# mLSTM and HGRN2 step on one Trainium2 core: the heads' normalised rows turned by VectorE and DRAM in place of TensorE

## The chip, the cores and the metric

One core of one Trainium2 chip. The metric is the time of one execution of the whole program on the device, in microseconds (us); three runs of the kernel before give a median of 1104.61 (1103.64 to 1105.09).

The engines named below work side by side, each through its own list of instructions in order: TensorE (PE; its weight loads are shown as PEld), VectorE (DVE), ScalarE (ACT), GpSimd (POOL) and SyncE (SP). SP issues nearly all DMAs here.

## The reference

One inference step of a layer with two parallel branches, for 512 prompt tokens and 32 sample tokens (544 together). Only the mLSTM branch matters here: four heads of 512 channels.

```python
def _head_layernorm(h, g):
    mu = jnp.mean(h, axis=-1, keepdims=True)
    d = h - mu
    y = d * lax.rsqrt(jnp.mean(d * d, axis=-1, keepdims=True) + EPS)
    return y.reshape(h.shape[0], h.shape[1], -1) * g
...
hm, C_new, n_new, m_new = _mlstm(qm, km, vm, ig, lf, C0, n0, m0)
hm = _head_layernorm(hm.transpose(0, 2, 1, 3), mnorm_g[l])
hm = (hm + m_skip[l] * c) * jax.nn.silu(z_m)
ya = hm.astype(x.dtype) @ w_brm[l]
```

c is the convolved and activated input of the head, z_m a gate, and ya the branch's output, summed over the heads. Everything is float32.

## The kernel before, in words

**Layout.** Nearly everything is held turned: channels on the 128 partitions, the 544 tokens along the free axis (32 sample tokens first, then 512 of the prompt), so a head is KH = 4 tiles f of 128x544. A product of float32 matrices is made of three matmuls: each operand is split into a high half (a cast on ACT, line 146 for rows, 204 for weights) and a low half (a subtraction on DVE, line 147 or 205). Names end in h and l: hm4h and hm4l are the halves of hm tile 4, ws210h and ws210l those of a sum of projection weights.

**Heads.** mchain(h, pump) computes head h = 0 to 3. It is a generator: each `yield n` lets `pump` put n steps of the *next* projection units on PE (line 575; six matmuls a step) before the head goes on. So PE's list is a mixture written by hand: a piece of the head, some projection, a piece of the head. The orders of ACT, DVE and SP come from the scheduler, by the program's order, its priorities and the times it reckons with; they are fixed when the program is built.

**The place that changes.** A head's output comes out with tokens on partitions: five tiles y, four of 128x512 (prompt) and one of 32x512 (sample). They are normalised in place, tiles 1 and 3 by ACT (line 1345), 0, 2 and 4 by DVE (line 1347). To meet c and z they must be turned to channels on partitions. For each f, five matmuls against the identity (lines 1366, 1367) write a PSUM tile yt, and DVE adds it, times the norm's weight, into c: line 1372 for the prompt, 1373 for the sample. Line 1374 multiplies by z, and split gives hm.

- Heads 1 and 2 first run memory(h, f) for their new state (96 matmuls, line 1112; the results Co go out by SP at line 1128) and then the projection steps KWGAP[2] = 11. Heads 0 and 3 wait GAPS[h] = 20 or 14 steps.
- stage_br(h) follows with the ya matmuls (line 229): eight units of 24 matmuls, each over all four hm tiles. A unit begins with hm tile 0 and the weights wbm; from head 1 on DVE adds earlier heads' sums (line 1392), which travel through DRAM (ya_d).
- Between a head's chain and its ya come the last projection units of that stage. Their weights are loaded by SP, cast by ACT and subtracted on DVE, in the same lists as the hm work.
- Behind head 3 the HGRN2 part begins. Its first activations tf, hq and hkq need three different function tables on ACT (ACT_TABLE_LOAD).

**Turning through DRAM is in the kernel already.** For heads 1 to 3 the rows kf are turned by `turn` (line 975: DVE transposes blocks of 32 by 32 in place; line 979: SP writes the blocks to DRAM, k_d, 16 DMAs a head), and read back at lines 1155 and 1164.

Of the kernel before, what the change touches and what calls it, by code (L numbers as in the profile page):

```python
# [9 lines left out]
F32 = mybir.dt.float32  # L10
# [4 lines left out]
ALU = mybir.AluOpType  # L15

P = 128
D = 1024
KD = D // P
NS = 32  # L20
NP = 512
T = NS + NP
TH = T // 2
FAR, NEAR = 48, 4
MH = 4
HD = 512
KH = HD // P
HH = 8
NB = NP // P
# [12 lines left out]
PDGAP = 1  # L42
VGAPS = (0, 0, 0, 0)
ZN = 3
FIRSTK, KTGAP, KWGAP = (3, 2, 1, 1, 1), (6, 14), (6, 3, 11)
VTGAP = ((2, 1, 1, 1, 1), (1, 1, 1, 1, 1), (1, 1, 1, 1, 1), (0, 2, 2, 1, 1))
GAPS = (20, 20, 20, 14)
APART = 10
FDELAY = (2, 2, 5)
QDELAY = 2  # L50
# [33 lines left out]
def hybrid_step(ctx: ExitStack, tc: tile.TileContext, a, o):  # L84
    nc = tc.nc
    V, S, G, PE = nc.vector, nc.scalar, nc.gpsimd, nc.tensor
# [20 lines left out]
    dr = ctx.enter_context(tc.tile_pool(name="dr", bufs=1, space=bass.MemoryType.DRAM))  # L107
    pd = ctx.enter_context(tc.tile_pool(name="pd", bufs=4, space=bass.MemoryType.PSUM))

    def slot(name, dt=F32):  # L110
        return sp.tile([P, WP + P // 2], dt, tag="s", name=name)
# [26 lines left out]
    def paux(name):  # L138
        return psum["a"].tile([P, 2, 512], F32, tag="a", name=name)
# [141 lines left out]
    ident = cp.tile([P, P], F32, name="ident")  # L281
# [822 lines left out]
    def memory(h, f, kw, vv, pool=paux):  # L1104
# [23 lines left out]
        nc.sync.dma_start(o["Cp"][h, f], co[:, :VW])  # L1128
        yield

    v_d = dr.tile([NB, 2, P, VW], F32, name="v_d")
    k_d = [dr.tile([T, HD], F32, name=f"k_d{h}") for h in range(MH)]

    def mchain(h, pump):

        t = st8[h]
# [69 lines left out]
        for b in range(NB):  # L1206
            yield VTGAP[h][b]
            pt = paux(f"vt{h}{b}")
# [10 lines left out]
        pt = paux(f"vts{h}")  # L1219
# [56 lines left out]
        yb = []  # L1276
        olds += [old(2), old(3)]

        def sample():
            pn = paux(f"nm{h}{NB}")  # L1280
            for f in range(KH):
                ch, cl = olds[f]
                last = f == KH - 1
                for g in range(2):
                    v, d = VS[g], slice(VP[g], VP[g] + VN[g])
                    if last:
                        PE.matmul(pn[:NS, g, d], dss, vs[:, v], start=False, stop=False)
                    for x, m in ((1, 1), (0, 2)) if last else ((0, 2), (1, 1)):
                        PE.matmul(
                            pn[: m * NS, g, d],  # L1290
                            qw[:, f, :m].rearrange("p o t -> p (o t)"),
                            (ch, cl)[x][:, v],
                            start=(f == 0 and x == 0),
                            stop=(last and x == 0),
                        )
            ysm = slot(f"y{h}{NB}")
            G.memset(ysm[:, :HD], 0.0)
            with tc.high_priority():
                S.copy(ysm[:NS, :VW], joined(pn)[:NS])
                yl = slot(f"yl{h}")  # L1300
                S.copy(yl[:NS, :VW], joined(pn)[NS : 2 * NS])
                V.tensor_tensor(ysm[:NS, :VW], ysm[:NS, :VW], yl[:NS, :VW], ALU.add)
                numbers(NB, NS, ysm)
            return ysm

        for i in range(NB):
            if i == NB - 1:
                ysm = sample()
# [13 lines left out]
            y = slot(f"y{h}{i}")  # L1322
# [5 lines left out]
        n5 = NB + 1  # L1328
        with tc.high_priority():
# [11 lines left out]
            for i in range(n5):  # L1341
                p = P if i < NB else NS
                y = yb[i][:p, :HD]
                if i % 2:
                    S.activation(y, y, AF.Identity, scale=rs[:p, i : i + 1], bias=mrs[:p, i : i + 1])
                else:
                    V.tensor_scalar(y, y, stt[:p, i, 0:1], rs[:p, i : i + 1], ALU.subtract, ALU.mult)

        if 0 < h < MH - 1:
            for b in range(NB):  # L1350
                fetch(b)
            yield KWGAP[0]
            for b in range(NB):
                parted(b)
            yield KWGAP[1]
            for f in range(KH):
                for _ in memory(h, f, kw, vv):
                    pass

        hs = []  # L1360
        for f in range(KH):
            yield max((KWGAP[2] if 0 < h < MH - 1 else GAPS[h]) if f == 0 else 1, pump.when["z", f] - pump.done)
            ft = h * KH + f
            pt = paux(f"yt{ft}")
            for b in range(NB):
                PE.transpose(pt[:, 0, b * P : (b + 1) * P], yb[b][:, f * P : (f + 1) * P], ident)
            PE.transpose(pt[:, 1, :P], yb[NB][:, f * P : (f + 1) * P], ident)
            c, (z, act) = t["cc"][f], t["z"][f]
            with tc.issue_after(act.ins):
                S.mul(c[:, :T], c[:, :T], vcol(V_SK + ft))  # L1370
            g = vcol(V_MG + ft)
            V.scalar_tensor_tensor(c[:, NS:T], pt[:, 0, :], g, c[:, NS:T], ALU.mult, ALU.add)
            V.scalar_tensor_tensor(c[:, :NS], pt[:, 1, :NS], g, c[:, :NS], ALU.mult, ALU.add)
            V.tensor_tensor(c[:, :T], c[:, :T], z[:, :T], ALU.mult)
            hs.append(split(c[:, :T], f"hm{ft}"))
        t["hs"] = hs
# [68 lines left out]
    with tc.manual_schedule(engines={mybir.EngineType.Activation, mybir.EngineType.DVE, mybir.EngineType.PE}):  # L1445
# [15 lines left out]
        for k in range(KD):  # L1461
            t = xt[k]
            hi, lo = far_pair("x0", k)
            g = t[:, T : T + 1]
# [10 lines left out]
            if k in (3, 4):  # L1475
                i = 2 * (k - 3)
                V.tensor_tensor(sq[i], sq[i], sq[i + 1], ALU.add)
            if k in (5, 6):
                i, j = ((0, 2), (4, 5))[k - 5]
# [9 lines left out]
        r = rms_cols(sq[0][:, :T], [(0, NS)] + [(NS + b * P, P) for b in range(NB)], "r0", pc)  # L1489
# [106 lines left out]
        pump = Pump(fill(0))  # L1596
# [103 lines left out]
    with tc.manual_schedule(engines={mybir.EngineType.PE}):  # L1700
        for h in range(MH):
# [16 lines left out]
            else:  # L1718
                pump = Pump(fill(h))
# [271 lines left out]
    with tc.manual_schedule(engines={mybir.EngineType.PE}):  # L1991
        pump = Pump(list(hgrn), staged=True)
# [17 lines left out]
    for k in range(2):  # L2010
        t = slot(f"p{k}")
# [46 lines left out]
    for k in range(KD // 2):  # L2058
        for f in (k, k + KD // 2):
            w = weight(a["w_brh"][f], f"wbh{f}", at=spread())  # L2060
            acc = dense(w, 0, P, P, obs, f"yb{f}")
            t = gbs[f]
# [191 lines left out]
```

## Time and profile before

| | |
|---|---|
| median of three runs | 1104.61 us |
| the profiled execution's own time | 1106.07 us |
| its span, first to last instruction | 1104.3 us |
| TensorE clock granted, mean | 0.999 |
| line 1366 and 1367, matmuls on PE | 64 and 16 |
| line 1112, matmuls of memory() | 288 |

Times in the rows are us from the span's start. A row of a timeline has start, length, engine, line, operation, output<-inputs, form and count, and in brackets how long the engine sat idle before it and what released it. A row of one tile or one line gives minimum, median and maximum of one instruction in ns, then the first and last start. A row of the waits is engine, tile and line, then what it waited for: total us, times, longest.

### The profile page before, as it was taken

How to read it: one execution, taken by the hardware profiler on the slowest of the kernel's cores; microseconds unless marked ns; L12 is line 12 of the kernel's file. 1: busy time of each engine (PE TensorE's matmuls, PEld its weight loads, DVE VectorE, ACT ScalarE, POOL GpSimd, SP SyncE). 2: the span in 40 equal slices, each digit the busy share in tenths (PEclk: the TensorE clock that was granted, in tenths of full speed). 3: DMA queues.
4: the chain of work that ended last, by engine and by line, in shares of the span. 5: the costliest groups of instructions: out<-in, count | busy, mean ns of one | idle time of the engine just before them, and what ended most of it. 6: DMA issues, size and time to landing. Idle time of an engine off the chain costs nothing.

```text
span 1104.3 us, 23737 instructions
## 1 busy us (share of the span) xinstructions
PE 1089.9 (99%) x8765; PEld 1077.4 (98%) x8765; DVE 920.8 (83%) x1989; ACT 712.2 (64%) x1571; POOL 173.0 (16%) x417
## 2 busy tenths in 40 slices
PE   9999999999999999999999999999999999999998
PEld 9999999999999999999999999999999999999998
DVE  6986999679798596986898688999999888789885
ACT  6686656755666455664566478887777767445762
POOL 2122024111010130101100123322332100000000
PEclk9999999999999999999999999999999999999999
DMA  6223225634365344464556222122221353343743
GB/s 224 78 96 107 83 86 174 146 100 127 105 206 160 81 147 144 126 225 92 157 159 218 95 78 84 56 80 80 85 75 62 111 178 116 116 124 116 260 146 121
DMA packets 104781, 138.67 MB, mean 126 GB/s; under 512 B 35765, under 2 KB 43573, under 8 KB 104665
## 3 DMA queue, kind: packets, MB, share of 16 engines
q1 hardware_dynamic: 104496, 137.10, 40.0%
q8 instruction: 69, 1.13, 0.4%
q14 instruction: 48, 0.39, 0.1%
q10 hardware_dynamic: 168, 0.06, 0.0%
HBM read 110.96 MB, written 26.16 MB: 124 GB/s over the span
## 4 chain that ended last, share of the span: by engine, by line
PE 59%; DVE 12%; ACT 7%; issue 2%; DMA 0%; POOL 0%; DVEq 0%; ACTq 0%; POOLq 0%
PE d L575 26%; PE ya L229 6%; PE pg L2099 4%; PE yb L229 4%; PE C L1112 3%; PE q L229 3%; DVE ws L533 2%; PE k L229 2%; PE sc L1054 2%; DVE hkq L1836 2%; PE nm L1313 2%; PE ple L229 1%; DVE at L1852 1%; DVE ws L508 1%; ACT shared L1947 1%
## 5 line engine op out<-in xcount | busy, mean ns | idle before, releaser
L592 ACT COPY t<-d 128x272 f32<-128x272 f32 x126 | 47.5, 377 | 20.8 <-PE d L575 20.7
L1770 ACT COPY kmos<-hkq 128x256 f32<-128x256 f32 x56 | 23.9, 427 | 38.0 <-DVE hkq L1836 34.7
L1836 DVE TENSOR_TENSOR hkq<-hkq,hq 128x288 f32<-128x288 f32 (+1 forms) x96 | 41.4, 438 | 1.5
L1815 PE MATMUL pl<-hkq,kmos 128*128 128x128 f32 x224 | 35.5, 279 | 3.3 <-DVE hkq L1653 1.9
L801 DVE SCALAR_TENSOR_TENSOR cv<-ub,vec,cv 128x547 f32<-128x547 f32 x48 | 37.1, 782 | 0.4
L1815 PEld LDWEIGHTS pl<-hkq,kmos 128*128 128x128 f32 x224 | 30.0, 188 | 4.9 <-ACT kmos L1770 1.5
L1112 PE MATMUL C<-vh,kwl 128*128 128x256 f32 x96 | 27.0, 281 | 0.0
L1112 PE MATMUL C<-vl,kwh 128*128 128x256 f32 x96 | 26.9, 280 | 0.0
L1112 PE MATMUL C<-vh,kwh 128*128 128x256 f32 x96 | 26.8, 279 | 0.0
L1392 DVE TENSOR_TENSOR y<-ya,y 128x272 f32<-128x272 f32 x48 | 18.8, 434 | 8.0 <-PE ya L229 7.8
L1852 DVE COPY_PREDICATED at<-lmask,pl 128x256 f32<-128x256 uint8 x56 | 25.0, 446 | 0.0
L1313 PE MATMUL nm<-vh,sh 128*128 128x256 f32 x80 | 22.8, 285 | 1.0 <-ACT Co L1124 0.6
L1324 ACT COPY y<-nm 128x516 f32<-128x516 f32 x16 | 9.4, 588 | 21.5 <-PE nm L1313 21.5
L1313 PE MATMUL nm<-vl,sh 128*128 128x256 f32 x80 | 22.6, 282 | 0.0
L963 POOL COPY vsm<-vt 128x96 f32<-128x96 f32 x16 | 12.8, 809 | 62.2 <-DVE vt L599 43.9
L1313 PE MATMUL nm<-vh,sl 128*128 128x256 f32 x80 | 22.5, 281 | 0.0
L1068 ACT CAST sh<-dm 128x512 fp32r<-128x512 f32 (+3 forms) x16 | 7.4, 459 | 22.8 <-DVE dm L1062 22.8
L1054 PE MATMUL sc<-q,kh 128*128 128x512 f32 (+3 forms) x80 | 18.6, 321 | 0.0
L1243 DVE SCALAR_TENSOR_TENSOR c<-c,wi,Cs 128x256 f32<-128x256 f32 (+1 forms) x32 | 14.9, 471 | 4.1 <-PE Cs L1241 4.0
L1112 PEld LDWEIGHTS C<-vh,kwh 128*128 128x128 f32 x96 | 18.1, 189 | 0.0
L1112 PEld LDWEIGHTS C<-vl,kwh 128*128 128x128 f32 x96 | 18.1, 188 | 0.0
L1112 PEld LDWEIGHTS C<-vh,kwl 128*128 128x128 f32 x96 | 18.0, 188 | 0.0
(5767 smaller groups left out, 5164.6 us busy)
## 6 DMA issues: line engine op xcount, KB each, us to landing
ya_d<-y SPq DMA_DIRECT2D x32, 272.0 KB, 3.1
y<-ya_d SPq DMA_DIRECT2D x24, 272.0 KB, 3.1
c<-in_C SPq DMA_DIRECT2D x16, 258.0 KB, 3.6
out_Cs<-c SPq DMA_DIRECT2D x16, 258.0 KB, 2.6
out_Cp<-Co SPq DMA_DIRECT2D x15, 258.0 KB, 2.5
k_d<-kf SPq DMA_DIRECT2D x48, 68.0 KB, 2.0
x<-in_xT SPq DMA_DIRECT2D x8, 272.5 KB, 4.6
ya<-ya_d SPq DMA_DIRECT2D x8, 272.0 KB, 4.7
```

The costliest lines, as they stand in the source:

```text
L229: PE.matmul(both[b][:m, :TH], part(w, off + k * step, m, x), xx[:, half(b)], start=(k == 0 and j == 0), stop=(k == n - 1 and j == 2),)
L575: PE.matmul(ps, ww[:, c], xx, start=(start and k == 0 and j == 0), stop=end, skip_group_check=not start,)
L592: S.copy(t, ps)
L801: last = V.scalar_tensor_tensor(cv[:, :547], ub[:, j : j + 547], vcol(V_CW + 4 * ft + j), cv[:, :547], ALU.mult, ALU.add)
L1054: PE.matmul(pn[:, 0, :n], ks[f][x][:, j * P : (j + 1) * P], qs[f][y][:, NS + j * P : T], start=(f == 0 and i == 0), stop=(f == KH - 1 and ...
L1112: PE.matmul(pn[g], kw[b][x][:, f * P : (f + 1) * P], vv[b][y][:, VS[g]], start=(b == 0 and j == 0), stop=(b == NB - 1 and j == 2),)
L1313: PE.matmul(pn[:, g, VP[g] : VP[g] + VN[g]], st[j][x][:, (i - j) * P : (i - j + 1) * P], vv[j][y][:, VS[g]], start=(j == 0 and q == 0), st ...
L1770: S.copy(km.rearrange("p (n j c) -> p n j c", j=2, c=c), view(kk, HB, ((2 * c, NA // (2 * c)), (c - HB, 2), (1, c))),)
L1815: PE.matmul(pn[:, b * P : (b + 1) * P].rearrange("p (n j c) -> p j n c", j=2, c=c), km[:, b * P : (b + 1) * P], view(qq, b * P, ((HB + c, ...
L1836: V.tensor_tensor(x, x, t, ALU.mult)
L1852: V.copy_predicated(blocks2(at[:, :NA]), twice(lmask[:, li, :P]), blocks2(pn[:, :NA]))
L2099: PE.matmul(ps, part(w, k * P, P, x), xx[:, c], start=(k == 0 and j == 0), stop=(k == KD - 1 and j == 2))
```

## The change

PE no longer turns y. Instead, for each head:

- DVE transposes each of the five y tiles in place, in blocks of 32 by 32 (V.transpose in turn_y).
- SP writes the blocks to their turned place in DRAM, y_d: one DMA for 32 rows, 64 KB in pieces of 128 bytes, 17 a head.
- SP reads four tiles yt of 128x544 back (turned_y, 272 KB each) into slots of the common ring of 26.
- DVE adds yt from SBUF in one instruction of 544 columns.

In heads 1 and 2 the turning and the writes stand ahead of memory(), the reads behind it. In heads 0 and 3 the tiles are turned one to a step. KWGAP[2] and GAPS give way to YGAP. A clearing of the sample tile's unused rows on POOL goes, since nothing reads them now. Lines of the changed kernel differ by up to 17 from those of before.

```diff
@@ -42,9 +42,8 @@
 PDGAP = 1
 VGAPS = (0, 0, 0, 0)
 ZN = 3
-FIRSTK, KTGAP, KWGAP = (3, 2, 1, 1, 1), (6, 14), (6, 3, 11)
+FIRSTK, KTGAP, KWGAP, YGAP = (3, 2, 1, 1, 1), (6, 14), (6, 3), (2, 4, 7)
 VTGAP = ((2, 1, 1, 1, 1), (1, 1, 1, 1, 1), (1, 1, 1, 1, 1), (0, 2, 2, 1, 1))
-GAPS = (20, 20, 20, 14)
 APART = 10
 FDELAY = (2, 2, 5)
 QDELAY = 2
@@ -1128,6 +1127,7 @@
         nc.sync.dma_start(o["Cp"][h, f], co[:, :VW])
         yield
 
+    y_d = [dr.tile([HD, T], F32, name=f"y_d{h}") for h in range(MH)]
     v_d = dr.tile([NB, 2, P, VW], F32, name="v_d")
     k_d = [dr.tile([T, HD], F32, name=f"k_d{h}") for h in range(MH)]
 
@@ -1294,7 +1294,6 @@
                             stop=(last and x == 0),
                         )
             ysm = slot(f"y{h}{NB}")
-            G.memset(ysm[:, :HD], 0.0)
             with tc.high_priority():
                 S.copy(ysm[:NS, :VW], joined(pn)[:NS])
                 yl = slot(f"yl{h}")
@@ -1346,6 +1345,20 @@
                 else:
                     V.tensor_scalar(y, y, stt[:p, i, 0:1], rs[:p, i : i + 1], ALU.subtract, ALU.mult)
 
+        def turn_y(i):
+            y, at = (yb[i][:, :HD], NS + i * P) if i < NB else (yb[i][:NS, :HD], 0)
+            V.transpose(y, y)
+            blocks = y_d[h].rearrange("(n e) t -> e n t", e=NS)
+            for r in range(0, y.shape[0], NS):
+                nc.sync.dma_start(blocks[:, :, at + r : at + r + NS], y[r : r + NS].rearrange("p (n t) -> p n t", t=NS))
+
+        def turned_y():
+            out = []
+            for f in range(KH):
+                out.append(slot(f"yt{h}{f}")[:, :T])
+                nc.sync.dma_start(out[f], y_d[h][f * P : (f + 1) * P, :])
+            return out
+
         if 0 < h < MH - 1:
             for b in range(NB):
                 fetch(b)
@@ -1353,24 +1366,28 @@
             for b in range(NB):
                 parted(b)
             yield KWGAP[1]
+            for i in range(n5):
+                turn_y(i)
             for f in range(KH):
                 for _ in memory(h, f, kw, vv):
                     pass
+        else:
+            yield YGAP[0]
+            for i in range(n5):
+                turn_y(i)
+                yield 1
+        yield YGAP[1]
+        yt = turned_y()
 
         hs = []
         for f in range(KH):
-            yield max((KWGAP[2] if 0 < h < MH - 1 else GAPS[h]) if f == 0 else 1, pump.when["z", f] - pump.done)
+            yield max(YGAP[2] if f == 0 else 1, pump.when["z", f] - pump.done)
             ft = h * KH + f
-            pt = paux(f"yt{ft}")
-            for b in range(NB):
-                PE.transpose(pt[:, 0, b * P : (b + 1) * P], yb[b][:, f * P : (f + 1) * P], ident)
-            PE.transpose(pt[:, 1, :P], yb[NB][:, f * P : (f + 1) * P], ident)
             c, (z, act) = t["cc"][f], t["z"][f]
             with tc.issue_after(act.ins):
                 S.mul(c[:, :T], c[:, :T], vcol(V_SK + ft))
             g = vcol(V_MG + ft)
-            V.scalar_tensor_tensor(c[:, NS:T], pt[:, 0, :], g, c[:, NS:T], ALU.mult, ALU.add)
-            V.scalar_tensor_tensor(c[:, :NS], pt[:, 1, :NS], g, c[:, :NS], ALU.mult, ALU.add)
+            V.scalar_tensor_tensor(c[:, :T], yt[f], g, c[:, :T], ALU.mult, ALU.add)
             V.tensor_tensor(c[:, :T], c[:, :T], z[:, :T], ALU.mult)
             hs.append(split(c[:, :T], f"hm{ft}"))
         t["hs"] = hs
```

**SP in head 1.** Before, from the first of the four state stores (Co10) to the first load of stage_br; wi and wbm are weight loads:

```order
L1128 DMA out_Cp<-Co10_4270 128x516
L172 DMA wi10r1_4450<-in_w_in 128x512
L172 DMA wbm10r0_4756<-in_w_brm 128x512
L1128 DMA out_Cp<-Co11_4298 128x516
L1128 DMA out_Cp<-Co12_4326 128x516
L1128 DMA out_Cp<-Co13_4354 128x516
L172 DMA wbm10r512_4758<-in_w_brm 128x512
L1386 DMA y100_4768<-ya_d_119 128x544
```

Now, behind the same wbm10r0:

```order
L1353 DMA y_d1_140<-y10_3980 32x16x32 x4
L1353 DMA y_d1_140<-y11_4006 32x16x32 x4
L1353 DMA y_d1_140<-y12_4041 32x16x32 x4
L1353 DMA y_d1_140<-y13_4111 32x16x32 x4
L1353 DMA y_d1_140<-y14_4066 32x16x32
L1127 DMA out_Cp<-Co11_4324 128x516
L1127 DMA out_Cp<-Co12_4352 128x516
L1127 DMA out_Cp<-Co13_4380 128x516
L1359 DMA yt10_4434<-y_d1_140 128x544
L1359 DMA yt11_4436<-y_d1_140 128x544
L1359 DMA yt12_4438<-y_d1_140 128x544
L1359 DMA yt13_4440<-y_d1_140 128x544
```

Seventeen writes stand ahead of the stores of Co11 to Co13, and the reads behind them. wbm10r512 follows the last read.

**DVE in head 1**, where the c chain meets the projection's weights (ub and z are projection results taken out of PSUM, ws and wa weights). Before:

```order
L205 TENSOR_TENSOR wa228l_4517<-wi9r1_3932,wa228h_4516 128x512
L599 TENSOR_TENSOR z12_3885<-d381_3884,t1638_4180 128x272
L205 TENSOR_TENSOR ws210l_4567<-ws210_4564,ws210h_4566 128x512
L1372 SCALAR_TENSOR_TENSOR c4_2508<-yt4_4480,vec_84,c4_2508 128x512
L599 TENSOR_TENSOR ub8_4371<-d81_4370,t18_4389 128x32
L599 TENSOR_TENSOR ub8_4371<-d81_4370,t18_4389 128x240
L1373 SCALAR_TENSOR_TENSOR c4_2508<-yt4_4480,vec_84,c4_2508 128x32
L1372 SCALAR_TENSOR_TENSOR c5_2670<-yt5_4502,vec_84,c5_2670 128x512
L1374 TENSOR_TENSOR c4_2508<-c4_2508,z10_3699 128x544
L1373 SCALAR_TENSOR_TENSOR c5_2670<-yt5_4502,vec_84,c5_2670 128x32
L1372 SCALAR_TENSOR_TENSOR c6_2756<-yt6_4526,vec_84,c6_2756 128x512
L147 TENSOR_TENSOR hm4l_4491<-c4_2508,hm4h_4490 128x544
```

Now; the sum c4<-yt10 and its product with z10 stand just ahead of this piece:

```order
L146 TENSOR_TENSOR hm4l_4518<-c4_2513,hm4h_4517 128x544
L598 TENSOR_TENSOR ub8_4397<-d81_4396,t18_4415 128x32
L598 TENSOR_TENSOR ub8_4397<-d81_4396,t18_4415 128x240
L1391 TENSOR_TENSOR c5_2675<-c5_2675,z11_3705 128x544
L1390 SCALAR_TENSOR_TENSOR c6_2761<-yt12_4438,vec_84,c6_2761 128x544
L1390 SCALAR_TENSOR_TENSOR c7_2847<-yt13_4440,vec_84,c7_2847 128x544
L146 TENSOR_TENSOR hm5l_4533<-c5_2675,hm5h_4532 128x544
L1391 TENSOR_TENSOR c6_2761<-c6_2761,z12_3890 128x544
L1391 TENSOR_TENSOR c7_2847<-c7_2847,z13_3891 128x544
L600 SCALAR_TENSOR_TENSOR ub9_4400<-d81_4396,t1678_4559 128x272
L146 TENSOR_TENSOR hm6l_4550<-c6_2761,hm6h_4549 128x544
L204 TENSOR_TENSOR ws210l_4573<-ws210_4570,ws210h_4572 128x512
```

ws210l stood ahead of the first sum, and stands behind hm6l. Head 2 has the same order with ws214l, c8 and hm10l.

**ACT in head 3**, where the casts of hm meet the first activations of HGRN2 (c14 is the product with the skip weight). Before:

```order
L146 CAST hm12h_8574<-c12_6807 128x544
L204 CAST wbm300h_8776<-wbm30r0_8772 128x512
L830 ACTIVATE z32_8142<-z32_8142 128x544
L1370 ACTIVATE c14_7059<-c14_7059,vec_84 128x544
L146 CAST hm13h_8600<-c13_6971 128x544
L204 CAST wbm301h_8780<-wbm30r512_8774 128x512
L204 CAST wbm310h_8850<-wbm31r0_8846 128x512
L592 COPY t16748_8691<-d480_8509 128x272
L204 CAST wbm311h_8854<-wbm31r512_8848 128x512
L146 CAST hm14h_8640<-c14_7059 128x544
L146 CAST hm15h_8664<-c15_7147 128x544
L603 ACTIVATE tf0_8512<-d480_8509 128x272
```

Now:

```order
L602 ACTIVATE tf0_8540<-d480_8537 128x272
L1659 ACT_TABLE_LOAD
L1659 ACTIVATE hkq0_8728<-tf0_8540 128x544
L1667 ACT_TABLE_LOAD
L1667 ACTIVATE hq0_8539<-hq0_8539 128x544
L1660 ACT_TABLE_LOAD
L1660 ACTIVATE tf0_8540<-tf0_8540 128x544
L1661 ACTIVATE hkq0_8728<-hkq0_8728,lc_149 128x544
L1662 ACTIVATE tf0_8540<-tf0_8540,lb_148,lc_149 128x544
L203 CAST wbm321h_8936<-wbm32r512_8930 128x512
L145 CAST hm12h_8641<-c12_6814 128x544
L145 CAST hm13h_8658<-c13_6978 128x544
```

All four casts hm12h to hm15h stood ahead of tf0. They stand behind three table loads, the five activations and the cast of wbm321. On DVE wbm321l, which needs that cast, stands directly ahead of the sum c12<-yt30 now.

In head 0 the list of DVE holds the splits of wbm00 and wbm01 ahead of the first sum now, and the loads of wbm00r512 and wbm01 stand behind the 17 writes on SP.

## The prediction

> **What bounds the kernel now.** The page comes first: how busy each engine is, and the chain that ended last. The engines' waits come second, to see whether TensorE ever waits for anything.
>
> ```profile
> span 1104.3 us, 23737 instructions
> ...
> PE 1089.9 (99%) x8765; PEld 1077.4 (98%) x8765; DVE 920.8 (83%) x1989; ACT 712.2 (64%) x1571; POOL 173.0 (16%) x417
> ...
> PE 59%; DVE 12%; ACT 7%; issue 2%; DMA 0%; POOL 0%; DVEq 0%; ACTq 0%; POOLq 0%
> ...
> PE pl L1815 <- DVE hkq L1653: 1.9, 5, 0.4
> PE warm L1451 <- DVE emc L1266: 1.1, 1, 1.1
> ```
>
> PE is busy 99% of the span, and its largest wait in total is 1.9 us in five pieces. So the kernel is a full queue of matmuls. Work taken out of that queue is saved in full, and each operand that comes late is lost in full, because nothing later has idle time that could take it up. Two things decide: what the 80 transposes cost PE, and whether the new way round delivers as early as PE asks.
>
> The profiled run took 1106.07 us, 1.5 above the median of 1104.61. I form the difference on the trace and add it to the median.
>
> **What goes from PE.** The timeline of PE around the first transposes of head 0:
>
> ```profile
> 158.44 0.29 PE L575 MATMUL d<-xfh,wa224h 128*128 128x272 f32 x1
> ...
> 159.19 0.60 PE L1366 MATMUL yt<-ident,y 128*128 128x128 f32 x4
> 159.63 0.27 PE L1367 MATMUL yt<-ident,y 128*128 128x128 f32 x1
> ...
> 160.49 0.60 PE L1366 MATMUL yt<-ident,y 128*128 128x128 f32 x4
> ```
>
> Six projection matmuls go from 158.44 to 159.19: 0.75. Five transposes and six such matmuls go from 159.19 to 160.49: 1.30. A group of five costs 0.55, four groups 2.2 in each head, sixteen **8.8 us**. That is the whole gain. From here on PE's demand comes 2.2 earlier than in the trace of before.
>
> **What comes on VectorE.** By tile and by line (min/median/max in ns):
>
> ```profile
> L1372 DVE SCALAR_TENSOR_TENSOR c<-yt,vec,c x16: 729/743/746, 160.5 to 584.7; 128x512 f32<-128x512 f32 x16
> L1373 DVE SCALAR_TENSOR_TENSOR c<-yt,vec,c x16: 229/243/249, 161.2 to 585.6; 128x32 f32<-128x32 f32 x16
> L1374 DVE TENSOR_TENSOR c<-c,z x16: 704/718/736, 162.0 to 587.0; 128x544 f32<-128x544 f32 x16
> ...
> L975 DVE STREAM_TRANSPOSE kf<-kf x12: 731/740/746, 203.3 to 503.7; 128x544 f32<-128x544 f32 x12
> ```
>
> Neighbours on DVE overlap by about 0.1, so a 0.72 instruction advances the queue by 0.62. The four big turnings of a head have a double in line 975 (0.74 for 544 columns); five, the last of them small, take about 3.2. The sum with yt becomes one instruction of 544 columns in place of two: I step it at 0.69, between line 1372 and the longer form, and 16 of line 1373 (0.24) go. The net is near +10 on an engine with 17% idle. In heads 1 and 2 it falls into idle time. I cost it at nothing beyond the chains below; without that cover it would be at most 3.2 a head.
>
> **What comes on SP and DRAM.** Line 979 writes blocks of the same form (turned 32 by 32, 128-byte runs), so k_d prices the new writes. Its tile, SP's timeline and the list of DMA issues (KB, us to landing):
>
> ```profile
> L979 SPq DMA_DIRECT2D k_d<-kf x48: 303/504/1302, 204.1 to 506.0; - x48
> ...
> DMA to landing us min/median/max: 1.7/2.4/6.2
> ...
> 204.10 11.32 SPq L979 DMA_DIRECT2D k_d<-kf x16
> 215.47 0.51 SPq L172 DMA_DIRECT2D wi22r<-in_w_in  x1
> ...
> 217.16 0.80 SPq L1164 DMA_DIRECT2D kr<-k_d  x2
> ...
> y<-ya_d SPq DMA_DIRECT2D x24, 272.0 KB, 3.1
> ...
> ya<-ya_d SPq DMA_DIRECT2D x8, 272.0 KB, 4.7
> ```
>
> One write steps SP by 0.504 and a gap of some 0.03, say 0.53 (bounds 0.30 and 1.30); from the first of 17 to the last are 16 steps, **8.5**. The last k_d write began at 215.42 − 0.51 = 214.91, and the read back at 217.16: **2.25** from the last write to the first read, which waits at the head of SP's queue. Weight loads and out_Cp stores stand behind it. A read of 272 KB lands 3.1 to 4.7 after issue; I take 3.5 for the first of four. So yt is there some 8.5 + 2.25 + 3.5 = 14.2 after the first write began; the PE transposes of a group took 0.55.
>
> The rule that speaks against such a path: the Trainium skill, "VectorE: DVE Perf Modes", section "The three transpose paths", calls a plain DMA copy that transposes by strides 19 times slower than the crossbar's 1309 ns for 128x128 bf16 when the innermost destination stride is large. As an estimate by that page 19 × 1.31 = 25 us for 32 KB, and 17 writes of 64 KB would end hundreds of us late. The k_d rows disagree: they have unbroken 128-byte runs, and 68 KB landed in 2.4 median. What is left of the rule is the congestion rival below.
>
> **Head 0.** When y is normalised, and when PE wants hm0:
>
> ```profile
> 151.18 1.44 DVE L1347 TENSOR_SCALAR y<-y,stat,rs 128x512 f32<-128x512 f32 x3
> ...
> 171.85 0.41 PE L229 MATMUL ya<-hm0h,wbm000h 128*128 128x272 f32 x2
> ```
>
> Normalised at 152.6; turnings from 153.0; the first write at 153.7, the last at 162.2. Three weight loads are issued in the 2.25 that follow; the read goes out at 164.5 and lands at 168.0. Then VectorE needs four sums (0.69), four products (0.62), four low halves (0.64) and the two weight splits between: 9.1, to 177.1. The last six of the 24 matmuls of the first ya unit follow (0.74): 177.8. Before, that unit ended at 171.85 + 24 × 0.124 = 174.8. Net **+3.0** (saving already in it).
>
> **Heads 1 and 2.** Here memory() hides most of the trip, and hm itself has time. What is late is a projection weight that VectorE now splits *behind* the c chain:
>
> ```profile
> 286.00 1.44 DVE L1347 TENSOR_SCALAR y<-y,stat,rs 128x512 f32<-128x512 f32 x3
> ...
> 299.63 0.43 DVE L599 TENSOR_TENSOR z<-d,t 128x272 f32<-128x272 f32 x1
> 299.98 0.68 DVE L205 TENSOR_TENSOR ws210l<-ws,ws210h 128x512 fp32r<-128x512 f32 x1
> ...
> L575 PE MATMUL d<-xfh,ws210l x4: 285/288/289, 308.8 to 309.9; 128*128 128x272 f32 x4
> ...
> 432.03 1.44 DVE L1347 TENSOR_SCALAR y<-y,stat,rs 128x512 f32<-128x512 f32 x3
> ...
> L575 PE MATMUL d<-xfh,ws214l x4: 285/288/289, 455.4 to 456.5; 128*128 128x272 f32 x4
> ```
>
> Before, ws210l was done at 300.7 and wanted at 308.8. Now: y at 287.4, the first write at 288.2, the last at 296.7, the read issued at 298.9, landed at 302.4. c4 waits for it, and ws210l stands behind c4 to hm6l: eleven large instructions 7.2, four evictions (0.43 as quoted, two of them shorter) 1.2, itself 0.6, together 9.0: ready at 311.4. PE asks at 308.8 − 2.2 = 306.6. Stall 4.8, net **+2.6**. Even if yt came at once, the queue is free at 300.05 (the row at 299.63), and 300.05 + 9.0 = 309.1 is 2.5 late: that bounds the term from below at +0.3. Head 2 has the same order, but 455.4 − 433.5 = 21.9 from y to the use instead of 21.4, 0.6 more with the second decimals: stall 4.2, net **+2.0**.
>
> **Head 3.** No memory stands between, and ScalarE's order changed: the hm casts now stand behind three table loads.
>
> ```profile
> 574.44 1.44 DVE L1347 TENSOR_SCALAR y<-y,stat,rs 128x512 f32<-128x512 f32 x3
> ...
> 587.36 0.29 PE L575 MATMUL d<-xfh,wa2248l 128*128 128x272 f32 x1
> ...
> 588.98 0.41 PE L229 MATMUL ya<-hm12h,wbm300h 128*128 128x272 f32 x2
> ...
> 588.34 0.39 ACT L603 ACTIVATE tf<-d 128x272 f32<-128x272 f32 x1
> 588.63 0.61 ACT L204 CAST wbm320h<-wbm32r 128x512 fp32r<-128x512 f32 x1
> 589.25 1.28 ACT L1642 ACT_TABLE_LOAD   x1
> ...
> 596.43 0.60 ACT L204 CAST wbm321h<-wbm32r 128x512 fp32r<-128x512 f32 x1
> ```
>
> From tf to the end of wbm321h took 597.0 − 588.3 = 8.7, with the wbm320h cast (0.5) in it that now comes earlier: 8.2. tf needs the matmuls that ended at 587.6, now 585.4: about 0.4 later it can start, so wbm321h is done at 594.0 and its low half, which stands ahead of c12 on VectorE, at 594.6. yt is not the later one: y at 575.9, first write 576.9, last 585.4, read at 587.6, landed at 591.1. From 594.6 the twelve instructions to hm15l take 7.9, one ScalarE cast between them 0.65, the last six matmuls 0.74: 603.9. Before, the unit ended at 588.98 + 2.97 = 591.95. Net **+12.0**, the largest term. In front of it PE stands from 586.8 to about 598.5.
>
> **The clock.** The windows at the end (PE busy, then the granted clock ahead of the DMA share), and PE's first rows:
>
> ```profile
> 1098.00:1100.00 2.00, 1.63 (x14) 1.42 (x12) 0.00 (x0) 0.70 (x2) 0.00 (x0) 1.00 0.83 284
> ...
> 1101.00:1102.00 1.00, 0.00 (x0) 0.00 (x0) 0.00 (x0) 0.00 (x0) 0.00 (x0) 0.80 1.01 358
> ...
> 1.10 3.78 PE L1451 MATMUL warm<-warm 128*128 128x128 f32 x16 [1.10 <-DVE emc L1266]
> 4.81 0.82 PE L355 MATMUL u<-x00h,wf0h 128*128 128x272 f32 x2
> ...
> 6.16 0.41 PE L355 MATMUL u<-x00h,wf0h 128*128 128x272 f32 x2
> ```
>
> PE's last work ended near 1099.6, and the mean of 0.80 over 1101 to 1102 puts the fall to half near 1101.6: two us of idling can be enough. At the start half pace lasted from 1.1 to about 5.9, so a fall costs at most half of that, 2.4; at least nothing. The start comes from a longer rest, so I take two thirds, 1.6. Heads 1, 2 and 3 stand still for 4 us or more in one piece, head 0 in smaller pieces: 3 × 1.6 = **+4.8**.
>
> The Trainium skill, "TensorE: Matmul & The Clock Gate", section "Part 1: The HAM clock gate", has a free-running window of about 3.4 us for both fall and return. By that page a fall costs 1.7, and pauses of 4.2 and 4.8 need not fill a window: 1.7 to 5.1 in place of my 4.8.
>
> **Sum.** 3.0 + 2.6 + 2.0 + 12.0 + 4.8 = +24.4; 1104.6 + 24.4 = **1129**. About 0.2%, 2.2 us, is what a measurement of this kernel can tell from no change.
>
> **Rivals.**
> (a) *All waits are covered, only the saving is left*: 1104.6 − 8.8 = 1095.8, **faster**. One mechanism: the c chain is done before PE asks, in every head. In head 1 it decides at 306.6 for ws210l, and VectorE's own queue already gives 309.1; in head 3 at 586.8 for hm12, and tf's table loads exclude that unless the order on the chip isn't the one listed. Chance 0.04.
> (b) *A quick trip*: writes step at 0.30, so yt lands 16 × 0.23 = 3.7 earlier and the clock holds. Head 0 −0.7, head 1 +0.3, head 2 −0.3, head 3 still +12.0: +11.3, 1116. The minimum of the k_d row speaks for it, its median against. Chance 0.10.
> (c) *Stalls as summed, but no fall of the clock*: 1104.6 + 19.6 = 1124. Chance 0.17; inside the range.
> (d) *Congestion*: 128-byte pieces beside weight loads; the write steps at 0.90, halfway to the row's 1.30. Each trip is 16 × 0.37 = 5.9 longer: heads 0 to 2 +17.7, head 3 (591.1 + 5.9 against 594.6) +2.4: 1149. Chance 0.07.
> (e) *Gain and stalls nearly cancel*: trips as in (b), and head 3's casts not held up by the table loads. Then yt30 lands at 587.4, its unit ends 9.3 later at 596.7, +4.8 there; −0.7 + 0.3 − 0.3 + 4.8 = +4.1, 1108.7. Half its cases, by what the sums are unsure of, would lie within 0.2%. Chance 0.07, 0.03 of it within.
> The forecast itself, 1121 to 1141: 0.55. The range takes in (b) and (c), and above it a fall of the clock at the full 2.4 in all four heads (+4.8) and reads landing in 4.7 instead of 3.5 in three heads (+3.6): 1129 + 8.4, and some for what I have not seen: 1113 to 1142. Faster 0.04, same 0.03, slower 0.93.
>
> **What would show it.** In the profile of the changed kernel PE should lose 80 matmuls and about 9 us of busy time, and its list of waits should hold four new lines: hm0 in head 0, ws210l and ws214l (released by VectorE's split) of 4 to 5 us, and hm12 near 14 in all, with ScalarE idle or in table loads ahead of it. k_d's price is wrong if the y_d writes step far from 0.53; the SP term is wrong if the first yt lands much before or after 14.2 us from the first write. The clock term is wrong if the granted clock stays at 1 behind those pauses. If ya in head 3 starts near 587, the largest term is gone, and with it most of the forecast.

## The result, and the profile after

The changed kernel takes 1133.23 us (median of five runs, 1131.28 to 1133.81) against 1104.61 (1103.64 to 1105.09): 1.0255 times, 95% interval 1.0241 to 1.0269. It is slower by 28.6 us; 1129 was forecast, in a range of 1113 to 1142. The profiled execution is the fastest of the five, 1131.28, 1.95 below their median; the profiled execution of before was 1.5 above its own. So the two traces lie 25.3 apart, and the medians 28.6.

The page of the changed kernel:

```profile
span 1129.6 us, 23706 instructions
...
PE 1091.1 (97%) x8685; PEld 1075.4 (95%) x8685; DVE 931.8 (82%) x1993; ACT 713.2 (63%) x1571; POOL 169.8 (15%) x413
...
PE 70%; DVE 16%; ACT 8%; issue 3%; DMA 1%; SPq 0%; POOL 0%; DVEq 0%; ACTq 0%; POOLq 0%
```

PE has 80 matmuls fewer, yet it is busy a little longer and idle for some 24 us more of the span. The prediction's sign, about 9 us less of busy time, does not show. Matmuls at half clock count as busy too, so busy time alone hides the saving: in the run saving below, where the granted clock is 1.00 throughout, PE is busy for 1079.6, 10.3 less than before. PE's waits (what waited, for whom, then total us, times, longest) say where the idle time lies:

```profile
PE ya L228 <- ACT hm12h L145: 10.7, 1, 10.7
PE d L574 <- DVE z L600: 7.2, 2, 3.9
PE ya L228 <- ACT hm0h L145: 5.0, 1, 5.0
...
PE d L574 <- DVE ws210l L204: 0.3, 1, 0.3
PE d L574 <- DVE ws214l L204: 0.3, 1, 0.3
```

There is one long pause in each head. In head 0 smaller pieces were forecast. In heads 1 and 2 the long one is for z, and not for the splits of ws210 and ws214, which have 0.3 each.

To size them, the same matmul is looked up in both traces (first start of its group by tile); for the two largest terms the rows are, before and after:

```profile
L229 PE MATMUL q<-cs4l,wq110h x4: 282/285/287, 214.4 to 217.5; 128*128 128x272 f32 x4
L228 PE MATMUL q<-cs4l,wq110h x4: 283/285/287, 220.3 to 223.4; 128*128 128x272 f32 x4
...
L229 PE MATMUL ya<-hm12h,wbm330h x4: 283/285/287, 606.8 to 609.8; 128*128 128x272 f32 x4
L228 PE MATMUL ya<-hm12h,wbm330h x4: 283/285/287, 632.2 to 635.3; 128*128 128x272 f32 x4
```

The difference of two neighbouring rows of the table is what lies between them, the 2.2 saved in each head included:

| first matmul on | before | after | later by | in between |
|---|---|---|---|---|
| wa224h, ahead of head 0's turning | 157.7 | 157.2 | -0.5 | |
| cs4l and wq110h, behind head 0 | 214.4 | 220.3 | 5.9 | head 0: +6.4 |
| ws210l, in head 1 | 308.8 | 318.9 | 10.1 | head 1: +4.2 |
| ws214l, in head 2 | 455.4 | 469.2 | 13.8 | head 2: +3.7 |
| hm12h and wbm330h, behind head 3's first ya units | 606.8 | 632.2 | 25.4 | head 3: +11.6 |

Forecast were 3.0, 2.6, 2.0 and 12.0, and 1.6 for the clock in each of the last three. Behind the last row nothing more is lost: the spans differ by 25.3.

**Head 0.** SyncE, then VectorE, of the changed kernel:

```profile
153.25 10.37 SPq L1353 DMA_DIRECT2D y_d<-y  x17
163.73 0.42 SPq L171 DMA_DIRECT2D wbm00r<-in_w_brm  x1
...
165.34 1.75 SPq L1359 DMA_DIRECT2D yt<-y_d  x4
...
169.29 0.44 DVE L598 TENSOR_TENSOR ub<-d,t 128x272 f32<-128x272 f32 x1 [2.48 <-PE d L574]
169.65 0.69 DVE L204 TENSOR_TENSOR wbm001l<-wbm00r,wbm001h 128x512 fp32r<-128x512 f32 x1
...
171.45 1.48 DVE L1390 SCALAR_TENSOR_TENSOR c<-yt,vec,c 128x544 f32<-128x544 f32 x2
...
179.88 0.73 DVE L146 TENSOR_TENSOR hm3l<-c,hm3h 128x544 fp32r<-128x544 f32 x1
```

The first sum (171.45) shows no wait of its own: it stands behind three weight splits, and these behind the eviction ub, which waits for PE's last projection matmul. The first yt was there before: the list of DMA issues, asked for 165.3 to 165.6 alone, gives it 4.6 us to land, so about 169.9. From the first sum to the end of hm3l (180.61) it is 9.2, as reckoned.

**Head 1.** SyncE, VectorE, and the use of ws210l on PE:

```profile
294.33 9.90 SPq L1353 DMA_DIRECT2D y_d<-y  x17
304.33 1.42 SPq L1127 DMA_DIRECT2D out_Cp<-Co  x3
305.97 1.85 SPq L1359 DMA_DIRECT2D yt<-y_d  x4
...
307.05 0.44 DVE L600 SCALAR_TENSOR_TENSOR z<-d,t 128x272 f32<-128x272 f32 x1 [1.44 <-DMA out_Cp<-Co]
309.18 0.81 DVE L1390 SCALAR_TENSOR_TENSOR c<-yt,vec,c 128x544 f32<-128x544 f32 x1 [1.68 <-DMA yt<-y_d]
...
L574 PE MATMUL d<-xfh,ws210l x4: 285/288/392, 318.9 to 320.1; 128*128 128x272 f32 x4
```

The stores of Co stand behind the 17 writes and go out at 304.3 only. The tile z takes over a place in the evictions' ring that a Co held, so z waits for a store to end; the PSUM tile that z empties stays taken, and PE stops for it (3.2 us). The first sum then waits for yt, and ws210l follows it as listed.

**Head 3.** ScalarE, VectorE, PE:

```profile
599.36 1.28 ACT L1659 ACT_TABLE_LOAD   x1
...
606.52 0.60 ACT L203 CAST wbm321h<-wbm32r 128x512 fp32r<-128x512 f32 x1
...
607.29 0.69 DVE L204 TENSOR_TENSOR wbm321l<-wbm32r,wbm321h 128x512 fp32r<-128x512 f32 x1
607.89 1.48 DVE L1390 SCALAR_TENSOR_TENSOR c<-yt,vec,c 128x544 f32<-128x544 f32 x2
...
610.74 0.82 PE L228 MATMUL ya<-hm12h,wbm300h 128*128 128x272 f32 x2 [10.74 <-ACT hm12h L145]
```

Table loads, the cast of wbm321, its split, the first sum: each right behind the one before, as forecast.

**DMAs and the clock.** From the list of DMA issues (KB, us to landing), and windows of head 0 (each with its length, then the busy time of PE, PEld, VectorE, ScalarE and GpSimd; the clock is the number ahead of the last two):

```profile
y<-ya_d SPq DMA_DIRECT2D x24, 272.0 KB, 2.9
y_d<-y SPq DMA_DIRECT2D x68, 64.0 KB, 1.9
yt<-y_d SPq DMA_DIRECT2D x16, 272.0 KB, 4.6
...
170.00:172.00 2.00, 0.00 (x0) 0.00 (x0) 2.00 (x4) 0.00 (x0) 1.58 (x3) 0.99 1.02 374
172.00:174.00 2.00, 0.00 (x0) 0.00 (x0) 2.00 (x4) 0.40 (x1) 0.00 (x0) 0.50 1.06 408
...
176.00:178.00 2.00, 2.00 (x10) 2.00 (x10) 2.00 (x4) 0.65 (x1) 0.00 (x0) 0.50 0.00 0
178.00:180.00 2.00, 1.73 (x9) 1.36 (x8) 2.00 (x5) 1.14 (x2) 0.00 (x0) 0.80 0.00 0
```

PE stops at 169.3; the clock is at half from about 172.0 and back at about 178.8. The clock falls to half in the other three heads too.

### The profile page after: what moved, and what is told of

It reads as the page before. It is cut to its first block, busy times and chain, and to the rows that moved or that the text cites. A ratio compares the mean times of both kernels' runs of the same rounds, so it can differ in the third digit from the quotient of the medians.

```text
span 1129.6 us, 23706 instructions
## 1 busy us (share of the span) xinstructions
PE 1091.1 (97%) x8685; PEld 1075.4 (95%) x8685; DVE 931.8 (82%) x1993; ACT 713.2 (63%) x1571; POOL 169.8 (15%) x413
## 4 chain that ended last, share of the span: by engine, by line
PE 70%; DVE 16%; ACT 8%; issue 3%; DMA 1%; SPq 0%; POOL 0%; DVEq 0%; ACTq 0%; POOLq 0%
PE d L574 27%; PE ya L228 8%; PE pg L2116 4%; PE yb L228 4%; PE k L228 4%; PE q L228 4%; PE C L1111 3%; DVE ws L532 2%; PE u L354 2%; PE sc L1053 2%; PE v L228 2%; DVE hkq L1853 2%; PE nm L1312 2%; PE d L454 1%; PE ple L228 1%
## 5 line engine op out<-in xcount | busy, mean ns | idle before, releaser
L792 POOL COPY uo<-ub 128x3 f32<-128x3 f32 x16 | 13.9, 871 | 31.4 <-DVE ub L600 20.1
```

## The experiments

Medians below stand beside runs of the kernel before on the same chip: 1104.76 for saving, h012, h12 and clock, 1103.88 for clock2, hm_first, h12_coact and h12_order, 1104.74 for two_h12 and two_after, 1104.59 for two_slot. Where runs of different groups are compared, the ratios are the safer guide.

**saving: the turning left out.** The sum reads z in place of yt, so the head's output lacks y.

```diff
-            V.transpose(y, y)
...
-                nc.sync.dma_start(blocks[:, :, at + r : at + r + NS], ...)
...
-                nc.sync.dma_start(out[f], y_d[h][f * P : (f + 1) * P, :])
...
-            V.scalar_tensor_tensor(c[:, :T], yt[f], g, c[:, :T], ALU.mult, ALU.add)
+            V.scalar_tensor_tensor(c[:, :T], z[:, :T], g, c[:, :T], ALU.mult, ALU.add)
```

> Left out: the turning of y altogether (no VectorE transposes, no y_d writes, no yt reads; the sum takes z in place of yt). Theory of the prediction: PE's queue is the bound, and 80 transposes cost it 8.8 us and nothing else; 1104.6 - 8.8 = 1095.8, between 1095 and 1097. Rival: without the transposes another engine or the clock becomes the bound, and less is saved: above 1099.

Measured 1094.68, ratio 0.9913 [0.9896, 0.9929]: 7.8 to 11.5 us less than before. The median is just below the 1095 to 1097 that were expected; the 8.8 lie in the interval. That PE is the bound and that the transposes cost it about 9 us holds. What the change loses elsewhere is then 28.6 + 8.8 to 10.1, some 37 to 39 us.

**h012 and h12: by heads.** The heads named in BYPE are turned by TensorE as before, with the gaps of before.

```diff
+BYPE = (3,)        # h12: (0, 3)
...
-            for i in range(n5):
-                turn_y(i)
+            if h not in BYPE:
+                for i in range(n5):
+                    turn_y(i)
...
+            if h in BYPE:
+                pt = paux(f"yt{ft}")
+                for b in range(NB):
+                    PE.transpose(pt[:, 0, b * P : (b + 1) * P], yb[b][:, f * P : (f + 1) * P], ident)
```

> Changed in heads 0, 1 and 2 alone; head 3 is turned by TensorE as before. Theory: each head pays for itself. By the trace of the changed kernel head 3 lost 12.5 net, so 1133.2 - 12.5 = 1120.7. Rival: the loss in head 3 is partly slack that the HGRN2 part behind it would have eaten anyway (its chain runs through VectorE): then the time falls by clearly less than 12.5, to 1125 or more.

> Changed in heads 1 and 2 alone. Theory: head 0 lost 6.4 net in the trace, so 1120.7 - 6.4 = 1114.3, and what is left over the time of before, 8 to 10, is heads 1 and 2. Rival (only the heads without memory between, 0 and 3, pay): 1104.6 - 4.4 = 1100.

Measured 1121.63 (1.0151 [1.0136, 1.0166]) and 1115.35 (1.0095 [1.0079, 1.0111]). Head 3 is worth 11.6, head 0 6.3, both as in the table of starts: each head pays for itself, and nothing behind it takes it up. Heads 1 and 2 alone are 10.6 slower than before in the medians, where the table has 7.9; the span of that run's profile is 1112.5, 8.2 above that of before, whose profiled execution took 1.5 more than its median.

**clock and clock2: PE kept busy in the pauses.** Added matmuls of the identity ahead of each pause; the lists of the other engines don't change.

```diff
+BUSY = (40, 26, 30, 88)     # clock2: (20, 13, 16, 46)
...
+        for _ in range(n):
+            PE.matmul(pn[:, :P], ident, ident, start=True, stop=True)
```

> The changed kernel, with 40, 26, 30 and 88 added matmuls of the identity by itself on PE ahead of the place where it waits in heads 0 to 3, so that it isn't idle there; the lists of VectorE, ScalarE and SyncE stay as they are. The granted clock should stay at 1 in all four places. The prediction's clock term (4.8): 1133.2 - 4.8 = 1128.4. Rival: PE's end of each place is set by the operand that comes last, and slow matmuls are slow only while it would wait anyway: 1133 within 1 us.

> As the run named clock, with half as many added matmuls (20, 13, 16, 46), since each took 0.22 us there and not the 0.11 that they were sized by, so that they end before the operand comes. The prediction's clock term (4.8): 1133.2 - 4.8 = 1128.4. Rival: the operand that comes last sets the end of each place: 1133 within 1 us.

clock took 1138.51 (1.0306 [1.029, 1.0321]). It was sized wrongly and says little: the view by tile of the added matmuls shows why.

```profile
L1137 PE MATMUL busy<-ident x368: 272/275/276, 169.9 to 622.1; 128*128 128x128 f32 x184
```

There are 368 records for 184 matmuls in the program: each is recorded as two and takes 0.22 in place of 0.11, and they ended past the operand, in head 0 4.4 later (ya began at 178.72, in the changed kernel at 174.30). clock2, with half as many, took 1134.26 (1.027 [1.0253, 1.0287]) against 1133.23: no gain. In heads 1 and 2 the clock then stayed at 1.00; the same stretch in the changed kernel and in clock2:

```profile
308.00:310.00 2.00, 2.00 (x13) 2.00 (x12) 0.81 (x1) 1.46 (x3) 0.61 (x4) 0.62 0.97 331
310.00:312.00 2.00, 2.00 (x11) 2.00 (x11) 1.98 (x4) 1.54 (x4) 0.00 (x0) 0.52 0.99 345
...
306.00:316.00 10.00, 10.00 (x86) 10.00 (x85) 7.13 (x13) 7.08 (x14) 0.81 (x5) 1.00 0.84 256
```

PE then reaches ws210l earlier and waits 1.6 there in place of 0.3. By the starts of the table's matmuls, clock2 is shorter than the changed kernel by 0.9 in head 1 and 0.1 in head 2, where 1.6 each was the price. In heads 0 and 3 the fall came a little later all the same (mean clock 0.87 and 0.84 over those stretches), when PE waited between the pieces of hm. It now lasted until 184.3 and 621.3, some 3.5 and 3.9 past the end of the last split of hm, where the changed kernel's clock was back before that end; these two heads are 1.5 and 1.7 longer. So a slow clock inside a wait costs little while a later operand sets the end, and one that reaches past the wait does cost. For head 0 the run clock agrees: at full clock throughout, its stretch is 63.0 against 63.1. What the fall costs in head 3 no run shows, since none has head 3 at full clock with the operand as the last thing to come.

**hm_first: head 3's casts ahead of the table loads.**

```diff
+        with tc.issue_after(made["hm15"].ins):
+            S.activation(kk[:, :T], tf[:, :T], AF.Sigmoid, scale=-1.0)
+            S.activation(q0[:, :T], q0[:, :T], AF.Silu)
+            S.activation(tf[:, :T], tf[:, :T], AF.Sigmoid)
```

> The changed kernel, with the five first activations of HGRN2 and their three table loads put behind the cast of hm15 on ScalarE. Theory of the prediction: the table loads set the start of the sums in head 3, but the way through DRAM is only a little shorter: yt30 was issued at 601.65, lands some 4.6 later at 606.2, the first sum began at 607.89; gain at most 1.7, 1131.5. Rival (the order of ScalarE is the whole cost of head 3): 1133.2 - 12 = 1121.

Measured 1131.53 (1.0247 [1.0231, 1.0262]): 1.7 less in the medians, but the ranges overlap (1129.82 to 1132.60 against 1131.28 to 1133.81) and the ratios differ by less than their intervals. In the traces head 3 is 0.1 shorter (from ws214l to wbm330h 162.9 against 163.0). What holds the sums now (SyncE, ScalarE, then VectorE of hm_first):

```profile
602.06 0.38 SPq L172 DMA_DIRECT2D wbm32r<-in_w_brm  x1
...
606.41 0.62 ACT L204 CAST wbm321h<-wbm32r 128x512 fp32r<-128x512 f32 x1 [6.49 <-DMA wbm32r<-in_w_brm]
...
607.07 0.69 DVE L205 TENSOR_TENSOR wbm321l<-wbm32r,wbm321h 128x512 fp32r<-128x512 f32 x1 [5.94 <-ACT wbm321h L204]
...
608.68 0.78 DVE L1391 SCALAR_TENSOR_TENSOR c<-yt,vec,c 128x544 f32<-128x544 f32 x1 [0.23 <-DMA yt<-y_d]
```

The cast of wbm321 no longer stands behind the table loads, but its weights have only just arrived: SP issues that load behind the 17 writes, which end at 600.94, and the reads of yt right behind it. The first sum (607.67) follows the split without a wait, and the second waits 0.23 for its yt. So in head 3 two chains end at almost the same time, the table loads and SP's queue of writes. Either alone makes the sums late, and taking one away wins next to nothing.

**two_h12 and two_after: the writes on two queues.**

```diff
-                nc.sync.dma_start(blocks[:, :, at + r : at + r + NS], ...)
+                q = nc.scalar if r // NS % 2 else nc.sync
+                q.dma_start(blocks[:, :, at + r : at + r + NS], ...)
```

> Heads 1 and 2 alone, with every second of the y_d writes issued by ScalarE and the others by SyncE, so that the stretch from the first write to the last is about half as long (some 5 us in place of 9.9) and the stores of Co and the reads behind it come 4 to 5 us earlier. Theory: the writes' issue on one queue is what makes heads 1 and 2 late: no wait for z, the first sum at about 298.5 on the axis of before, the split of ws210 at 307.5 against 306.6; some -1 a head against before: 1101 to 1106, where this kernel without the second queue took 1115.4. Rival: VectorE's list, not the way through DRAM, sets the end: above 1112.

> The kernel of the run hm_first (all four heads), with every second y_d write issued by ScalarE. Theory: heads 1 and 2 fall back by some 3 to 5 us each as in the run two_h12; in head 3 the first sum has to wait for the reads alone, which land 4 to 5 earlier; in head 0 it stands behind the last projection results in VectorE's list (ub7), so less is won there: 1131.5 - 8 - 4.5 - 1 = 1118, between 1114 and 1122. Rival (the writes' issue is not what is late): 1130 or more.

two_h12 took 1110.89 (1.0054 [1.0039, 1.0069]), 4.5 less than h12; two_after 1124.82 (1.0187 [1.0173, 1.0202]), 6.7 less than hm_first; by the starts of the table's matmuls 1.2, 2.0, 1.5 and 2.6 in heads 0 to 3. The writes' issue on one queue is a cause in both, but the gain is short of what was expected (1101 to 1106, 1114 to 1122). In two_h12, head 1:

```profile
286.69 6.48 SPq L1358 DMA_DIRECT2D y_d<-y  x9
...
299.71 0.79 DVE L1407 SCALAR_TENSOR_TENSOR c<-yt,vec,c 128x544 f32<-128x544 f32 x1 [0.58 <-DMA yt<-y_d]
```

Nine writes still took 6.5, 0.72 each, and the eight of ScalarE stood in its list between copies that wait for PE (1.62, 1.15 and 0.90), so that its last write went out only by 293.6; casts now come behind them. PE waited for z 4.0 in all in place of 8.0.

**h12_coact, h12_order, two_slot: the wait for z taken away.** h12_coact gives the stores of Co to ScalarE's queue; h12_order does that and puts VectorE's list in the order of the program from the first sum on, with a longer gap ahead of it; two_slot is two_h12 with Co in the common ring.

```diff
# h12_coact, h12_order
-        nc.sync.dma_start(o["Cp"][h, f], co[:, :VW])
+        (nc.scalar if 0 < h < MH - 1 else nc.sync).dma_start(o["Cp"][h, f], co[:, :VW])
# h12_order
-YGAP = (2, 4, 7)
+YGAP = (2, 4, 12)
+        with tc.manual_schedule(engines={mybir.EngineType.DVE, mybir.EngineType.PE}) if 0 < h < MH - 1 else nullcontext():
# two_slot
-        co = (eslot if h < MH - 1 else slot)(f"Co{h}{f}")
+        co = (eslot if h == 0 else slot)(f"Co{h}{f}")
```

> Heads 1 and 2 alone, and ScalarE issues their Co stores in place of SyncE, so these no longer stand behind the 17 writes. Theory: PE's wait for the z eviction (8.0 us in the run of heads 1 and 2) is gone, but the sums c4 to c7 still have to come late: the scheduler now lists them behind the splits of wbm10 and wbm11, which leaves 9 us of VectorE work after PE has reached ya, so the wait moves to ya: 1112 to 1120. Rival: the stores were the whole cause, 1115.4 - 8 = 1107.4.

> As h12_coact, and VectorE's list in this part is in the order of the program, with the first sum one step behind the split of ws210 (YGAP[2] is 12). Theory: no wait for z, none for ws210; but VectorE was full from 300 to 318 us before, the split of ws310 had 0.5 us to spare there, PE now comes 2.2 earlier and VectorE has only 0.6 less to do, and it begins 2 us later: ws310 3 us late, net +1 a head, 1105 to 1109. Rival: only the order and the stores were at fault: 1104.6 - 4.4 = 1100.2.

> The kernel of the run two_h12 (heads 1 and 2 alone, writes on two queues), with the state tiles Co of heads 1 and 2 in the common ring of 26 slots and not in the evictions' ring of 8, so that the tile z no longer waits for their stores. Theory: the wait for z (4.0 us in two_h12) goes; the sums start when yt lands, near 299 on the axis of before, and the split of ws210 behind them is done about 1 us after PE asks; net -1 a head: 1102 to 1107, perhaps just below before. Rival (the wait for z only stands in front of the later wait for the split, and nothing is won): 1110 to 1112.

Measured 1121.81 (1.0156 [1.014, 1.0171]), 1126.61 (1.0203 [1.0188, 1.0218]) and 1115.86 (1.0097 [1.0074, 1.012]). Each is slower than the kernel that it was made from (h12, h12_coact, two_h12). The longest waits of PE, first rows of the three runs in this order:

```profile
PE ya L230 <- ACT hm4h L147: 4.6, 1, 4.6
...
PE d L576 <- DVE ub L602: 12.2, 2, 6.6
...
PE d L576 <- DVE ws210l L206: 3.7, 1, 3.7
```

z is gone from the top each time, and another wait has its place. In h12_coact the sums are late for ya, as expected, but by more than reckoned (1112 to 1120): VectorE's list changed with the queue, and its first sum starts at 318.27, behind the splits of wbm10 and wbm11, where it started at 302.87 in h12. h12_order, expected at 1105 to 1109, missed by far. Its VectorE:

```profile
302.56 0.69 DVE L206 TENSOR_TENSOR ws210l<-ws,ws210h 128x512 fp32r<-128x512 f32 x1 [0.69 <-ACT ws210h L205]
306.45 0.79 DVE L1407 SCALAR_TENSOR_TENSOR c<-yt,vec,c 128x544 f32<-128x544 f32 x1 [3.19 <-DMA yt<-y_d]
```

ws210l is early now, but the first sum stands still for yt, and with it an eviction that PE waits for. In two_slot the freed z let the scheduler list other evictions, which wait for PE, ahead of the splits (ws38l began at 300.3; at 294.3 in two_h12), and the split of ws210 was 3.7 late. The reads of yt went out 4.2 later too (300.36 against 296.16): SP waited 4.2 for the writes, of which ScalarE's last stood behind waits for PE (2.59 and 1.09). So none of the three isolates the wait for z: the order of a list moved with it each time. What the stores of Co cost is read from the traces and is not shown by a run of its own. No version tried beats the kernel before.

## Why the prediction was right

**The bound and the gain.** Right: about 9 us on PE (saving), and what a head loses is lost in full (h012, h12).

**VectorE's turnings.** Right: five in one row, 3.06, where 3.2 were reckoned, and no wait of PE comes from them.

**The price of the trip.** Close: 17 writes took 9.9 to 10.5 (0.58 to 0.62 each, 0.53 reckoned) and reads landed in 4.6 median (3.5 taken). In head 1 it was 309.18 - 294.33 = 14.9 from the first write to the first sum; 14.2 were reckoned. The rule of the Trainium skill ("VectorE: DVE Perf Modes", section "The three transpose paths"), 19 times slower where the innermost destination stride is large, does not bear on this form: 64 KB in unbroken runs of 128 bytes landed in 1.9.

**Head 0.** Mis-sized: +6.4 for +3.0. The step that failed is "the read goes out at 164.5 and lands at 168.0. Then VectorE needs" 9.1, in two parts. The landing came 1.9 later, at about 169.9: the writes took 0.61 each, and the read 4.6 in place of 3.5. And the sums were started at the landing, but they start 1.5 behind it, at 171.45, after three splits which follow the eviction that waits for PE's last projection matmul. The list had been read, but only its length was used, not when its head is free. That the splits stand there because their loads moved behind the writes is likely; no run tested it.

**Heads 1 and 2.** The time was close and the first wait wrong. ws210l was ready at 318.9; the forecast 311.4, moved by the 6.3 by which y is normalised later (VectorE's row of it starts at 292.25, before at 286.00), is 317.7. Of the 1.2 that are missing the trip has 0.7 (14.9 for 14.2), and VectorE 0.6 (9.6 for 9.0 from the first sum to the end of that split); net the two heads cost +4.2 and +3.7 for +2.6 and +2.0. But the prediction named the split as the only stall and had put the stores of Co behind the writes at nothing, though it named them. They stop z, z stops PE, and PE's wait for the split is then almost used up (0.3). That the first sum waited for yt afterwards (1.68) shows, in this trace, that the trip set the start of the sums, and not the wait for z.

**Head 3.** Right: the order of the waits, the table loads, +11.6 for +12.0. But the table loads are not the only cause. The prediction had yt 3.5 ahead of the split of wbm321 (591.1 against 594.6), and did not count that the load for wbm321 stands behind the writes too. hm_first won 0.1 in that head: without the table loads, SP's queue makes the sums as late.

**The clock.** Wrong in its price, though the fall itself was foreseen: half clock in all four heads. Where it could be held off (clock2), 1.0 was won of the 3.2 priced for heads 1 and 2. Windows of half a us show when it fell and came back, here in heads 0 and 1 of the changed kernel:

```profile
171.50:172.00 0.50, 0.00 (x0) 0.00 (x0) 0.50 (x2) 0.00 (x0) 0.08 (x1) 0.96 1.03 391
178.50:179.00 0.50, 0.50 (x5) 0.50 (x4) 0.50 (x2) 0.14 (x1) 0.00 (x0) 0.71 0.00 0
...
308.00:308.50 0.50, 0.50 (x6) 0.50 (x5) 0.00 (x0) 0.50 (x2) 0.30 (x2) 1.00 1.01 374
308.50:309.00 0.50, 0.50 (x4) 0.50 (x3) 0.00 (x0) 0.50 (x2) 0.00 (x0) 0.50 1.05 305
311.50:312.00 0.50, 0.50 (x4) 0.50 (x4) 0.50 (x2) 0.50 (x2) 0.00 (x0) 0.59 0.86 316
```

A mean of 0.96 is 0.04 us at half clock, and so on: the slow stretches run from 171.96 to 178.79 and from 308.50 to 311.91, and by the same view from 458.68 to 462.10 and from 602.04 to 615.70. They last 6.83, 3.41, 3.42 and 13.66, which is 2, 1, 1 and 4 times 3.41, and their starts lie 136.54, 150.18 and 143.36 apart, which is 40, 44 and 42 times 3.41. The Trainium skill ("TensorE: Matmul & The Clock Gate", section "Part 1: The HAM clock gate") has a free-running window of about 3.4 for fall and return; the trace agrees with its length and with its running free of the kernel. A pause shorter than that was enough: in head 1 PE stood still for 3.24 and had been at work again for 0.95 when the clock fell.

**The sum.** +24.4 was forecast, +25.3 is the difference of the spans and +28.6 that of the medians. That the spans come so close is partly luck: the 4.8 for the clock stand in for 3.4 missing in head 0 and 3.3 in heads 1 and 2, less 0.4 too much in head 3 and the 0.5 by which PE was earlier ahead of head 0.

## What to carry to other kernels

Work taken off the engine that bounds is worth its full time only if what replaces it arrives before the first use: count from the last producer through issue, landing and reading back to the *place in the list* of the instruction that uses it, and ask when everything ahead of that place is free. Ask as well what was moved behind the new transfers on their queue, and whose buffer waits for it; here stores of finished results stopped PE. When two chains make an operand late, take both away before you judge either (head 3). A slow clock inside a wait costs little while another operand is late; one that reaches past the wait is paid for.

## What the runs showed of the hardware

A float32 128x128 matmul against the identity is recorded as two, and a row of them takes 0.22 us for each matmul of the program (clock). Reads of 272 KB from y_d landed in 4.6 where the same size read from ya_d into y took 2.9 (medians of the changed kernel); why isn't shown. Issuing a DMA from a second queue did not halve the stretch: 9 writes took 6.5 on SyncE beside 8 on ScalarE (two_h12), against 9.9 for 17 on one (h12). The half clock lasted whole multiples of 3.41 us, with starts whole multiples of 3.41 apart (changed kernel).
